# Per-page decode attention on Trainium2: the samples' softmax steps tied to pages, their small matrix products joined to the rope products, the constants and one split cut in parts

## The chip, the core and the metric

The kernel runs on one core of a Trainium2 chip. A core has five engines with instruction queues of their own: TensorE (PE, matrix products; its weight loads are listed apart as PEld), VectorE (DVE), ScalarE (ACT), GpSimd (POOL) and SyncE (SP, which here mostly issues DMAs). They meet through semaphores. The metric is the device time of one execution in microseconds (us), lower is better; the time of a kernel is the median of several runs.

## What is computed

One inference step of a one-layer decoder trunk, for a prompt of 512 tokens and, with the same weights, for 8 samples of one new token each (520 tokens in all; d_model 1024, everything float32). Each sample has 4096 past positions in 32 pages of 128, found through a page table. Cut to what the change concerns:

```python
def keys_nope(c, w_uk, k_norm_w):                 # a key per head from the 128-wide latent c
    return rmsnorm(jnp.einsum('bkr,rhd->bkhd', c, w_uk), k_norm_w)

def attend(q_nope, q_rope, k_nope, k_rope, c, w_uv, q_pos, k_pos):
    s = (jnp.einsum('bqhd,bkhd->bhqk', q_nope, k_nope)
         + jnp.einsum('bqhd,bkd->bhqk', q_rope, k_rope)).astype(jnp.float32) * SCALE
    s = jnp.where(k_pos[None, :] <= q_pos[:, None], s, -jnp.inf)
    p = jax.nn.softmax(s, axis=-1).astype(c.dtype)
    o_lat = jnp.einsum('bhqk,bkr->bqhr', p, c)
    return jnp.einsum('bqhr,rhd->bqhd', o_lat, w_uv)

# a sample: its 4096 cached latents and rope keys, then its own new token
past_c = cache_c[pages].reshape(past_len, KV_RANK)        # KV_RANK 128
past_r = cache_r[pages].reshape(past_len, QK_ROPE)        # QK_ROPE 32
c_all = jnp.concatenate([past_c, cn], axis=0)[None]

# the layer
z = hn @ w_in                        # q_lat, c_kv, k_r, u, v
sg = chunk_mix(u, v, w_s, b_s)       # the gated result, 512 wide
h = x + jnp.concatenate([attn, sg], axis=-1) @ w_o
# then a convolutional FFN (w_ff_in, w_ff_out) and a gate (w_ple_gate)
```

There are 8 heads, so a page of 128 positions gives 128 x 8 keys, each of 64 elements and normalised by its own mean square.

## The kernel before

**Arithmetic.** A large product is made of three products (`mm3`, L145 to L148): each operand is split into a rounded high part (a CAST on ACT, L135) and a remainder (a subtraction on DVE or POOL, `sub`, L130), and high x high, high x low and low x high are added in PSUM. Small products are made directly in float32, which PE does in two passes each.

**Stages.** The projections of q and the latent run to about 30 us of the span, the remaining projections and the gating to about 122, the prompt's attention in 16 blocks to about 205. Between these blocks the first sample's pages are worked on, two to a block. From 205 to 414 only pages are left, those of samples 1 to 7. From there on come the output projection (`o_half`), the FFN and the gate, to the end.

**A page** (`s_page`, L718 to L757; all 256 of them in order, 32 to a sample, 4 to a group). PE multiplies the page's latents by the key weights, six passes of 260 columns (`mm<-wuk,a`, two calls of `mm3`); 256 columns are keys, the last 4 are their products with the query. ACT squares the keys (L750) and copies the 4 columns to `raw` (L751), DVE sums the squares per head into `ss` (L752). PSUM for keys has three buffers (`mm`), the small products share two others (`ms`); the squares have three buffers, and `ss`, `raw` and the scores `sc` two each, one for each of two samples in turn. At the first page of a group the latents of a later group are split (`s_split`: CAST on ACT or POOL in turn, L714, subtraction on POOL, L130), and its rope keys are gathered by an indirect DMA that POOL issues (L588).

**Rope products.** At pages 0, 8, 16 and 24 of a sample the rope part of two groups' scores is made: 8 small products by `mm_cols` (L150 to L154), that is 16 passes on PE (`ms<-qbd,wr`), in four column tiles of 32, and one ACT copy of 64 columns into `sc` (L742).

**A sample's softmax** is a Python list of steps (`s_softmax`, L759). It is put into the list `steps` when the sample's last page has been issued, and `s_pages` (L859) takes one step from it after each page of the following sample from the fourth on: `var` (a POOL step, L792, and Ln on ACT), `rstd` (two ACT steps), the Newton correction, the sum of the scores, and the maximum per partition (all DVE); `mx_t` (L780) transposes the maxima on PE, `mx_all` reduces them on DVE, `mx_b` spreads them by a product (L789), then subtraction, Exp and sum. Behind page 23 `s_pv` (L819) issues probabilities times latents, 32 small products of 128 columns in 64 passes (L826, called PV here), and one more for the new token's own latent (L828, contraction over 8 rows of `cnew`). Then `s_out` copies that to SBUF and `s_fin` (L838) adds the four column tiles up and sums the denominators, by two `mm_cols` of 8 columns.

A scheduler sets the final order on each engine; `tc.issue_after` keeps an instruction behind another one.

**Other places.** The constants (`cst`, 128 x 1389) come in one DMA (L274), issued by SP among those of x and the first weights. The gated result `sgr` (2 tiles of 2 x 520 columns) is split for the output projection behind group 60 (L940), with the subtraction of each tile in one POOL instruction of 1040 columns. Behind the last page, what remains in `steps`, and `s_pv`, `s_out` and `s_fin` of sample 7 stand ahead of the output projection's (L968 on), the scheduler puts them among its products.

## Time and profile before

| | us |
|---|---|
| median of 3 runs (range) | 915.95 (913.79 to 916.31) |
| the profiled execution | 914.99 |
| its span, from first to last instruction | 913.1 |
| mean granted clock of PE in it | 0.991 of full |
| busy: PE, DVE, ACT, POOL | 894.5, 642.0, 505.1, 217.6 |

Everything below that names a place in time goes by microseconds from the span's start. A timeline row has the start, the busy time, engine, line, operation, and the tiles written and read; a number in brackets at its end is the idle time of the engine just before, with what ended it. Passes on PE overlap, as they are pipelined, so how fast PE goes is read from the difference between the starts of two rows, not from their durations. A group row has the number of instructions behind an x.

### The profile page before, as it was taken

How to read it: one execution, taken by the hardware profiler on the slowest of the kernel's cores; microseconds unless marked ns; L12 is line 12 of the kernel's file. 1: busy time of each engine (PE TensorE's matmuls, PEld its weight loads, DVE VectorE, ACT ScalarE, POOL GpSimd, SP SyncE). 2: the span in 40 equal slices, each digit the busy share in tenths (PEclk: the TensorE clock that was granted, in tenths of full speed). 3: DMA queues.
4: the chain of work that ended last, by engine and by line, in shares of the span. 5: the costliest groups of instructions: out<-in, count | busy, mean ns of one | idle time of the engine just before them, and what ended most of it. 6: DMA issues, size and time to landing. Idle time of an engine off the chain costs nothing.

```text
span 913.1 us, 20541 instructions
## 1 busy us (share of the span) xinstructions
PE 894.5 (98%) x7799; PEld 848.2 (93%) x7799; DVE 642.0 (70%) x1093; ACT 505.1 (55%) x1196; POOL 217.6 (24%) x240
## 2 busy tenths in 40 slices
PE   8998999999999999999999999999999999999997
PEld 6996878889999899889999999999999999999997
DVE  6679676668888898787668776337776337776775
ACT  6683368777887788785346443224443224455561
POOL 5005841238777677740000000000000000000000
PEclk9998999999999999999999999999999999999999
DMA  6332150352766556313333222322222322323311
GB/s 219 99 96 82 56 177 1 100 148 84 211 180 204 168 172 202 110 48 122 93 101 109 93 93 70 116 93 94 88 86 82 104 89 88 104 86 99 117 59 59
DMA packets 65203, 100.43 MB, mean 110 GB/s; under 512 B 13825, under 2 KB 47754, under 8 KB 65106
## 3 DMA queue, kind: packets, MB, share of 16 engines
q1 hardware_dynamic: 63058, 94.93, 32.8%
q0 software_dynamic: 2048, 4.20, 1.7%
q8 instruction: 62, 1.02, 0.5%
q14 instruction: 35, 0.29, 0.1%
HBM read 95.95 MB, written 3.15 MB: 109 GB/s over the span
## 4 chain that ended last, share of the span: by engine, by line
PE 86%; DVE 6%; ACT 3%; issue 1%; DMA 1%; SPq 1%; POOL 0%; ACTq 0%
PE mm L146 26%; PE mm L148 25%; PE mm L147 25%; DVE ss L752 2%; PE ms L826 2%; PE ms L693 1%; ACT sq L750 1%; PE ms L153 1%; ACT wr L666 1%; PE ms L146 1%; PE ms L641 1%; PE mm L658 1%; PE mm L678 1%; PE ms L148 1%; PE ms L147 1%
## 5 line engine op out<-in xcount | busy, mean ns | idle before, releaser
L146 PE MATMUL mm<-u,w 128*128 128x260 f32 x1392 | 395.1, 284 | 0.0
L148 PE MATMUL mm<-u,w 128*128 128x260 f32 x1392 | 394.5, 283 | 0.0
L147 PE MATMUL mm<-u,w 128*128 128x260 f32 x1392 | 393.5, 283 | 0.0
L147 PEld LDWEIGHTS mm<-u,w 128*128 128x128 f32 x1392 | 262.1, 188 | 0.4 <-issue 0.2
L148 PEld LDWEIGHTS mm<-u,w 128*128 128x128 f32 x1392 | 262.0, 188 | 0.1
L146 PEld LDWEIGHTS mm<-u,w 128*128 128x128 f32 x1392 | 261.8, 188 | 0.4 <-PE mm L148 0.2
L752 DVE TENSOR_REDUCE ss<-sq 128x8 f32<-128x512 f32 x256 | 168.0, 678 | 34.6 <-ACT sq L750 32.5
L130 DVE TENSOR_TENSOR w<-wr,w 128x1024 fp32r<-128x1024 f32 (+1 forms) x94 | 112.7, 1200 | 104.7 <-issue 54.1
L135 ACT CAST w<-wr 128x1024 fp32r<-128x1024 f32 (+1 forms) x94 | 96.5, 1031 | 135.9 <-PE mm L148 127.5
L750 ACT ACTIVATE sq<-mm 128x512 f32<-128x512 f32 x256 | 152.7, 609 | 25.5 <-PE mm L148 15.9
L146 PE MATMUL mm<-wuk,a 128*128 128x260 f32 x416 | 123.7, 297 | 1.8 <-ACT raw L751 1.8
L147 PE MATMUL mm<-wuk,a 128*128 128x260 f32 x416 | 118.7, 285 | 0.0
L148 PE MATMUL mm<-wuk,a 128*128 128x260 f32 x416 | 118.5, 285 | 0.0
L146 PEld LDWEIGHTS mm<-wuk,a 128*128 128x128 f32 x416 | 79.1, 190 | 4.9 <-ACT raw L751 3.1
L147 PEld LDWEIGHTS mm<-wuk,a 128*128 128x128 f32 x416 | 79.1, 190 | 0.1
L148 PEld LDWEIGHTS mm<-wuk,a 128*128 128x128 f32 x416 | 79.0, 190 | 0.0
L588 POOL DMA_INDIRECT wr<-krT,idx x64 | 62.8, 982 | 18.7 <-PE mm L678 7.4
L1069 ACT ACTIVATE a<-abuf,cst 128x512 f32<-128x512 f32 x44 | 35.9, 816 | 39.2 <-DVE abuf L1067 39.2
L130 POOL TENSOR_TENSOR a<-u,a 128x512 fp32r<-128x512 f32 x34 | 44.7, 1315 | 30.7 <-ACT a L714 28.5
L1070 DVE SCALAR_TENSOR_TENSOR a<-abuf,cst,a 128x512 f32<-128x512 f32 x44 | 33.0, 751 | 25.4 <-ACT a L1069 25.1
L751 ACT COPY raw<-mm 128x8 f32<-128x8 f32 x256 | 44.3, 173 | 0.0
L135 ACT CAST u<-a 128x520 fp32r<-128x520 f32 x24 | 14.8, 626 | 43.4 <-DVE a L1108 43.3
(306 smaller groups left out, 1341.0 us busy)
## 6 DMA issues: line engine op xcount, KB each, us to landing
wr<-w_ffi SPq DMA_DIRECT2D x44, 512.0 KB, 3.2
u<-pages SPq DMA_DIRECT2D x152, 128.0 KB, 2.6
w<-pages SPq DMA_DIRECT2D x104, 128.0 KB, 2.5
wr<-w_ffo SPq DMA_DIRECT2D x16, 512.0 KB, 3.3
wr<-w_o SPq DMA_DIRECT2D x8, 512.0 KB, 3.2
wr<-w_pg SPq DMA_DIRECT2D x8, 512.0 KB, 3.4
wr<-w_ffo SPq DMA_DIRECT2D x8, 384.0 KB
a<-xT SPq DMA_DIRECT2D x8, 260.0 KB, 6.2
```

The source lines that it names most:

```text
L130: return (nc.vector if eng == "v" else nc.gpsimd).tensor_sub(dl, src, dh.bitcast(F32))
L135: nc.scalar.copy(dh, src)
L146: nc.tensor.matmul(out, lh, rh, start=start, stop=False)
L147: nc.tensor.matmul(out, lh, rl, start=False, stop=False)
L148: return nc.tensor.matmul(out, ll, rh, start=False, stop=stop)
L588: nc.gpsimd.indirect_dma_start(krT[:, g * 128:(g + 1) * 128], None, I["krT"], bass.IndirectOffsetOnAxis(ap=idx.bitcast(U32)[:, b * 8 + g:b ...
L750: squares.append(nc.scalar.activation(u3(sq, 2, 256), ps[:, :, 0:256], AF.Square))
L751: nc.scalar.copy(raw[:, c * 8:c * 8 + 8].rearrange("p (a h) -> p a h", a=2), ps[:, :, 256:260])
L752: nc.vector.tensor_reduce(ss[:, c * 8:c * 8 + 8], sq.rearrange("p (h d) -> p h d", d=DN), axis=AX.X, op=ALU.add)
L826: nc.tensor.matmul(po[q:q + 32, 0:128], scp[:, c * 8:c * 8 + 32], pg[c // 4][:, c % 4, 128:256], start=(c < 4), stop=(c >= 29), tile_posit ...
L1069: nc.scalar.activation(c[:, 0:T], a[:, 2:T + 2], AF.Identity, scale=cw[:, m, 2:3], bias=cw[:, m, 3:4])
L1070: nc.vector.scalar_tensor_tensor(c[:, 0:T], a[:, 1:T + 1], cw[:, m, 1:2], c[:, 0:T], op0=ALU.mult, op1=ALU.add)
```

## The change

Six edits.

1. `KRQ` goes from 2 to 4: rope products are made at pages 0 and 16 of a sample only, for four groups at once, 16 products in 32 passes, held behind the preceding page's keys, with one ACT copy of 128 columns.
2. `steps` is a dict from page to step (page 4 `var`, 5 `rstd`, 6 to 9 the DVE steps, 17 `mx_all`, 20 `mx_b`, 21 subtraction, 23 Exp, 24 sum, 27 `s_pv`, 29 `s_out`).
3. `mx_t` is called by the rope products of page 16, right behind them, and `s_fin` by those of page 0 of the next sample but one, through the dict `with_qbd`.
4. The new token's product moves from `s_pv` to `s_fin`: `cnew` is padded with zeros to 128 rows and `mm_cols` adds four products of 8 columns to the same PSUM tile. PV's first product is held behind the keys before it.
5. The constants come in two DMAs, 685 columns behind all of x and the first weights, and 704 behind these.
6. The split of `sgr` goes in four pieces of 520 columns, behind groups 51, 54, 59 and 62.

```diff
-KRQ = 2
+KRQ = 4
+SGS = (51, 54, 59, 62)
...
-    def mm_cols(out, lhsT, rhs):
+    def mm_cols(out, lhsT, rhs, start=True, stop=True):
...
-        if j == 1:
-            nc.sync.dma_start(cst, I["cst"])
+    nc.sync.dma_start(cst[:, 0:NEARLY], I["cst"][:, 0:NEARLY])
...
+    nc.sync.dma_start(cst[:, NEARLY:], I["cst"][:, NEARLY:])
...
-    cnew = const([8, 128], F32, "cnew")
+    cnew = const([128, 128], F32, "cnew")
+    nc.gpsimd.memset(cnew, 0.0)
...
             for i in range(KRQ):
-                mm_cols(pr[:, 32 * i:32 * i + 32], krT[:, (g + i) * 128:(g + i + 1) * 128],
-                        qbd[:, b].rearrange("p j h -> p (j h)"))
+                with ExitStack() as es:
+                    if kmms:
+                        es.enter_context(tc.issue_after(kmms[-1].ins))
+                    r = mm_cols(pr[:, 32 * i:32 * i + 32], krT[:, (g + i) * 128:(g + i + 1) * 128],
+                                qbd[:, b].rearrange("p j h -> p (j h)"))
+            f = with_qbd.pop(g * 4, None)
+            if f:
+                f(r)
...
-        def mx_t():
+        def mx_t(after=None):
             hold["t"] = ms()
-            after_keys(lambda: nc.tensor.transpose(hold["t"][:8, 0:128], m1[:, 0:8], ident))
+            with tc.issue_after((after or kmms[-1]).ins):
+                nc.tensor.transpose(hold["t"][:8, 0:128], m1[:, 0:8], ident)
...
+        with_qbd[16] = mx_t
+        steps.update({
+            4: var,
+            5: rstd,
...
+            27: lambda: s_pv(b),
+            29: lambda: s_out(b),
+        })
...
-            nc.tensor.matmul(po[q:q + 32, 0:128], scp[:, c * 8:c * 8 + 32], pg[c // 4][:, c % 4, 128:256],
-                             start=(c < 4), stop=(c >= 29), tile_position=(0, q))
-        nc.tensor.matmul(po[0:32, 0:128], scp[:8, 256:288], cnew, start=False, stop=True, tile_position=(0, 0))
-        bst[b] = (po, psum)
+            with ExitStack() as es:
+                if c == 0:
+                    es.enter_context(tc.issue_after(kmms[-1].ins))
+                nc.tensor.matmul(po[q:q + 32, 0:128], scp[:, c * 8:c * 8 + 32], pg[c // 4][:, c % 4, 128:256],
+                                 start=(c < 4), stop=(c >= 28), tile_position=(0, q))
+        bst[b] = (po, psum, scp)
+        with_qbd[0] = lambda after: s_fin(b, after)
...
-        with tc.issue_after(kmms[-1].ins):
-            mm_cols(pt_[:, 0:8], ol, sel)
+        with tc.issue_after(after.ins):
+            mm_cols(pt_[:, 0:8], ol, sel, stop=False)
+        mm_cols(pt_[:, 0:8], cnew, scp[:, 256:264], start=False)
         mm_cols(pt_[:, 8:16], ones, psum[:, 0:8])
...
-            if steps and cur[0] % 32 > 3:
-                f = steps.pop(0)
-                if f:
-                    f()
+            f = steps.pop((cur[0] - 1) % 32, None)
+            if f:
+                f()
...
-        if g == 5:
-            s_pv(b - 1)
-            steps.extend([None, lambda b=b: s_out(b - 1), None, None, lambda b=b: s_fin(b - 1)])
...
-        if n == 60:
-            sgh, sgl = split_all(sgr, "g")
+        if n in SGS:
+            i, k = divmod(SGS.index(n), 2)
+            if k == 0:
+                sgh += pair(1, F32R)
+                sgl += pair(1, F32R)
+            split(sgh[i][:, k], sgl[i][:, k], sgr[i][:, k], l="g")
```

What this moves, word for word from the order of instructions on an engine. A row has the line, the operation, the tile written, the tiles read, and the shape; an x count folds equal rows. `mm` is a key PSUM tile, `wuk` the key weights, `a` a page's split latents, `ms` a PSUM tile of the small products, `wr` the gathered rope keys.

PE before the change, in the pages of sample 5: the transpose of sample 4's maxima (L782) stands alone between two pages' keys.

```order
L147 MATMUL mm_5380<-wuk_568,a_5148 128x260
L148 MATMUL mm_5380<-wuk_567,a_5149 128x260
L782 MATMUL ms_5356<-cst,s_5130 8x128
L146 MATMUL mm_5393<-wuk_567,a_5148 128x260
L147 MATMUL mm_5393<-wuk_568,a_5148 128x260
```

And a few pages on, at page 16, the rope products of two groups (L153), alone again.

```order
L147 MATMUL mm_5415<-wuk_568,a_5148 128x260
L148 MATMUL mm_5415<-wuk_567,a_5149 128x260
L153 MATMUL ms_5446<-qbd,wr_4739 32x32 x8
L146 MATMUL mm_5456<-wuk_567,a_5228 128x260
L147 MATMUL mm_5456<-wuk_568,a_5228 128x260
```

PE after the change at page 16 of sample 5 (L149 to L151 are `mm3`'s lines there, L156 is `mm_cols`): four groups' rope products and the transpose, L794, stand in one place.

```order
L150 MATMUL mm_5403<-wuk_570,a_5126 128x260
L151 MATMUL mm_5403<-wuk_569,a_5127 128x260
L156 MATMUL ms_5433<-qbd,wr_4730 32x32 x16
L794 MATMUL ms_5450<-cst,s_5108 8x128
L149 MATMUL mm_5453<-wuk_569,a_5228 128x260
L150 MATMUL mm_5453<-wuk_570,a_5228 128x260
```

The transpose has moved from a gap of its own to the rope products' gap, which holds twice as many of them.

PE before, behind page 23 of sample 5: the end of sample 4's PV, the new token's product (L828), and the rope products of page 24.

```order
L826 MATMUL ms_5566<-u_4593,sc_4533 32x128 x4
L826 MATMUL ms_5566<-w_4662,sc_4533 32x128 x4
L828 MATMUL ms_5566<-cnew,sc_4533 32x128
L153 MATMUL ms_5619<-qbd,wr_4739 32x32 x8
L146 MATMUL mm_5629<-wuk_567,a_5376 128x260
L147 MATMUL mm_5629<-wuk_568,a_5376 128x260
```

PE after, at page 0 of sample 5: four groups' rope products, then the final sums of sample 3, with the new token's product (`cnew`) among them.

```order
L151 MATMUL mm_5096<-wuk_565,a_4810 128x260
L156 MATMUL ms_5135<-qbd,wr_4730 32x32 x16
L156 MATMUL ms_5152<-cst,sq_5083 32x8 x4
L156 MATMUL ms_5152<-sc_3892,cnew 32x8 x4
L156 MATMUL ms_5152<-s_4490,ones 32x8 x4
L149 MATMUL mm_5169<-wuk_569,a_4894 128x260
L150 MATMUL mm_5169<-wuk_570,a_4894 128x260
```

The new token's product has left PV's end, the rope products of page 24 are gone from there, and the final sums no longer have a gap of their own.

POOL before, in the first pages of sample 7: a piece of the gated result's split (`u` 128x1040) and then, behind others, the variance step of sample 6 (L792).

```order
L130 TENSOR_TENSOR u_6713<-u_1036,u_6712 128x1040
L130 TENSOR_TENSOR a_6312<-u_6125,a_6311 128x512
L588 DMA wr_5981<-krT,idx 128x128
L714 CAST a_6390<-u_6222 128x512
L1056 MEMSET abuf_7543 128x2
L1056 MEMSET abuf_7545 128x2
L130 TENSOR_TENSOR a_6391<-u_6222,a_6390 128x512
L588 DMA wr_5981<-krT,idx 128x128
L792 TENSOR_SCALAR ss_5773<-ss_5773 128x256
```

POOL after, the same place (L133 is `sub`, L804 the variance step): two pieces of 520 columns.

```order
L133 TENSOR_TENSOR u_6643<-u_1039,u_6642 128x520 x2
L719 CAST a_6372<-u_6190 128x512
L1069 MEMSET abuf_7541 128x2
L1069 MEMSET abuf_7543 128x2
L133 TENSOR_TENSOR a_6373<-u_6190,a_6372 128x512
L735 MEMSET sc_6378 128x24
L736 COPY sc_6378<-snall 128x8
L592 DMA wr_5970<-krT,idx 128x128
L804 TENSOR_SCALAR ss_5750<-ss_5750 128x256
```

The piece of 1040 columns ahead of the variance step has become two of 520, the other two pieces lie earlier, and the set-up of `sc` (L735, L736) has moved to there.

More of the change, by code (lines that the diff above doesn't have):

```diff
@@ L34 @@
 NCONST = 1389
+NEARLY = 685
 NEG = -1.0e30
@@ L111, in trunk_step @@
     ident = take(128)
+    sel = take(8)
+    sel_last = take(8)
+    assert off[0] == NEARLY
     trilT = take(128)
@@ L115, in trunk_step @@
     row8 = take(272)
-    sel = take(8)
-    sel_last = take(8)
     gqk8 = row8[:8, 0:128].rearrange("p (a d) -> p a d", a=2)
@@ L404, in trunk_step @@
             qlat[t] = q
-    nc.gpsimd.tensor_copy(cnew, ctok[:8, 4])
+    nc.gpsimd.tensor_copy(cnew[:8], ctok[:8, 4])
     w5 = "p (t f) -> p t f"
@@ L701, in trunk_step @@
     bst = {}
+    steps, with_qbd = {}, {}
     def s_split(n):
@@ L756, in s_page @@
                 pages[b] = (None, pg)
-                steps.extend(s_softmax(b))
+                s_softmax(b)
     def s_softmax(b):
@@ L835, in s_out, with s_fin @@
             nc.scalar.copy(ol, po[:, 0:128])
-        bst[b] = (ol, psum)
-    def s_fin(b):
-        ol, psum = bst.pop(b)
+        bst[b] = (ol, psum, scp)
+    def s_fin(b, after):
+        ol, psum, scp = bst.pop(b)
         pt_ = ms()
-        with tc.issue_after(kmms[-1].ins):
-            mm_cols(pt_[:, 0:8], ol, sel)
+        with tc.issue_after(after.ins):
+            mm_cols(pt_[:, 0:8], ol, sel, stop=False)
+        mm_cols(pt_[:, 0:8], cnew, scp[:, 256:264], start=False)
         mm_cols(pt_[:, 8:16], ones, psum[:, 0:8])
@@ L846, in s_fin @@
         nc.vector.tensor_mul(olT[:, :, b], pt_[:, 0:8], rc[:, 0:8])
-    cur, steps = [0], []
+    cur = [0]
     def split_all(tiles, l):
@@ L928, in trunk_step @@
     k_pg = [wq_add(I["w_pg"][m], 1024) for m in range(8)]
+    sgh, sgl = [], []
     while cur[0] < 256:
@@ L966, in o_half @@
                 last(m, xv)
-    for f in steps:
-        if f:
-            f()
-    s_pv(7)
-    s_out(7)
-    s_fin(7)
+    with_qbd.pop(0)(kmms[-1])
+    steps[16] = with_qbd.pop(16)
+    for k in sorted(steps):
+        steps[k]()
+    with_qbd.pop(0)(kmms[-1])
     ps = ms()
```

38 lines of the change are left out of this document (14 added, 24 removed).

## The prediction

> **What bounds the kernel now.** I read the profile's first page, then the chain of waits, then PE's timeline around each small product in the sample stage.
>
> ```profile
> span 913.1 us, 20541 instructions
> PE 894.5 (98%) x7799; PEld 848.2 (93%) x7799; DVE 642.0 (70%) x1093; ACT 505.1 (55%) x1196; POOL 217.6 (24%) x240
> PE 86%; DVE 6%; ACT 3%; issue 1%; DMA 1%; SPq 1%; POOL 0%; ACTq 0%
> ```
>
> PE is busy for 98% of the span and makes up 86% of the chain. Only what shortens PE's own line can shorten the kernel: fewer passes, fewer pauses between passes, or a wait of PE. "Busy" hides pauses, since the records of pipelined passes overlap; they show in the starts. The chain in order of time gives the rhythm of the sample stage, by each sample's probability-times-latent product (PV, L826):
>
> ```profile
> 224.97 1.89 PE ms L826 x64
> 372.81 1.88 PE ms L826 x62
> 405.60 1.88 PE ms L826 x64
> 424.80 1.89 PE ms L826 x64
> ```
>
> From PV(0) at 224.97 to PV(5) at 372.81 lie five periods, 29.57 us each. The sixth, to 405.60, is 32.79, which is 3.22 more for the same work. One regular period by engine, and the rhythm of passes around one rope batch:
>
> ```profile
> 263.60:293.10 29.50, 29.00 (x348) 26.93 (x341) 24.93 (x45) 23.90 (x79) 21.31 (x24) 1.00 0.73 214
> 269.49 0.28 PE L148 MATMUL mm<-wuk,a 128*128 128x260 f32 x1
> 269.70 0.33 PE L153 MATMUL ms<-qbd,wr 128*32 128x32 f32 x16
> 269.96 0.39 PE L146 MATMUL mm<-wuk,a 128*128 128x260 f32 x1
> 270.18 0.28 PE L147 MATMUL mm<-wuk,a 128*128 128x260 f32 x1
> 270.30 0.29 PE L148 MATMUL mm<-wuk,a 128*128 128x260 f32 x1
> ```
>
> The first row gives the window, its length, then busy time of PE, PEld, DVE, ACT and POOL, the clock, the DMA share and GB/s. DVE is next behind PE, 24.93 of 29.50. Key passes start 0.12 apart (270.18 to 270.30). Across the rope batch the second pass behind it (270.18) starts 0.69 after 269.49, where two steps would be 0.24: the break costs 0.45. I price all breaks in this way, last key pass before to the second one behind.
>
> **The change part by part.**
>
> *Joined small products.* The same measure at a batch of 8 passes (sample 6's last), at the transpose of the maxima (L782), at the two early passes of PV, at the new token's product with the rope batch behind it, and at the final sums (s_fin):
>
> ```profile
> 397.80 0.27 PE L153 MATMUL ms<-qbd,wr 128*32 128x32 f32 x8
> 397.99 0.39 PE L146 MATMUL mm<-wuk,a 128*128 128x260 f32 x1
> ...
> 273.52 0.28 PE L148 MATMUL mm<-wuk,a 128*128 128x260 f32 x1
> 274.30 0.27 PE L782 MATMUL ms<-cst,s 128*8 128x128 f32 x1 [0.50 <-DVE s L805]
> 274.40 0.36 PE L146 MATMUL mm<-wuk,a 128*128 128x260 f32 x1
> 274.60 0.29 PE L147 MATMUL mm<-wuk,a 128*128 128x260 f32 x1
> ...
> 281.80 0.28 PE L148 MATMUL mm<-wuk,a 128*128 128x260 f32 x1
> 282.01 0.41 PE L826 MATMUL ms<-u,sc 128*32 128x128 f32 x2
> 282.57 0.28 PE L147 MATMUL mm<-wuk,a 128*128 128x260 f32 x1
> ...
> 285.85 0.40 PE L828 MATMUL ms<-cnew,sc 8*32 8x128 f32 x2
> 286.18 0.33 PE L153 MATMUL ms<-qbd,wr 128*32 128x32 f32 x16
> 286.44 0.39 PE L146 MATMUL mm<-wuk,a 128*128 128x260 f32 x1
> ...
> 290.00 0.28 PE L148 MATMUL mm<-wuk,a 128*128 128x260 f32 x1
> 290.22 0.25 PE L153 MATMUL ms<-cst,sq 128*32 128x8 f32 x8
> 290.30 0.23 PE L153 MATMUL ms<-s,ones 128*32 128x8 f32 x8
> 290.69 0.28 PE L147 MATMUL mm<-wuk,a 128*128 128x260 f32 x1
> ```
>
> From the start of a rope batch to the next key pass it is 0.26 with 16 passes (269.70 to 269.96) and 0.19 with 8 (397.80 to 397.99): 0.009 for a pass, so nearly all of a break is for going over and back, not for what is done there. Breaks of a regular period before: rope batches at pages 0, 8 and 16, 3 x 0.45; the transpose 1.08 - 0.24 = 0.84, of which 0.50 is a wait for DVE; the early PV passes 0.77 - 0.24 = 0.53, less 0.06 that two passes cost inside PV's own run (1.88 for 62); the token's product 0.33 and the rope batch behind it 0.26; the final sums 0.69 - 0.24 = 0.45. Together 3.70.
>
> After the change two such places are left. At page 0 there are 32 rope passes and 24 of the final sums (8 more for the new token, now in s_fin): 0.45 + 40 x 0.009 = 0.81. At page 16 there are 32 rope passes and the transpose: 0.45 + 16 x 0.009 + 0.10 (274.30 to 274.40) = 0.69. Together 1.50, so 2.20 is saved in a regular period. Pinning PV's first pass behind the keys keeps its 64 passes in one run; the break of mx_b stays.
>
> [...]
>
> *What is late next.* The steps of the softmax, on DVE and ACT, stand on the same pages as before, give or take one; pages now come faster, 24.93 of DVE work in about 27.4. Where DVE trails, a key product waits for a free PSUM buffer. Pauses that are taken from pages 0 to 15 (0.45 at page 8 and 0.84 at the transpose) may come back there, as waits: between 0 and 1.29. I take 0.30, nearer to nothing, because in the regular period PE shows a single wait, 0.50, and DVE still has 9% to spare. Net 1.90 a period.
>
> *The rope copies* go from four of 64 columns to two of 128 on ACT, with 23.90 busy of 29.50: nothing. A batch now needs four gathers of rope keys rather than two:
>
> ```profile
> 282.76 0.95 POOL L588 DMA_INDIRECT wr<-krT,idx  x1
> wr<-krT,idx POOLq DMA_INDIRECT x64, 2.9
> ```
>
> The fourth of the next sample is issued at 282.76 and lands some 2.9 later, at 285.7; that sample's page 0 is at 293.1, the end of the window quoted. 7 us to spare: 0.
>
> *The gated result's split.* Here lies the sixth period's surplus:
>
> ```profile
> 379.36 2.45 POOL L130 TENSOR_TENSOR u<-u,u 128x1040 fp32r<-128x1040 f32 x1 [3.23 <-DMA wr<-w_o]
> 387.40 0.41 POOL L792 TENSOR_SCALAR ss<-ss 128x256 f32<-128x256 f32 x1
> ...
> 389.37 0.39 PE L146 MATMUL mm<-wuk,a 128*128 128x260 f32 x1 [1.63 <-ACT raw L751]
> ...
> 391.20:394.60 3.40, 3.40 (x18) 3.40 (x18) 3.40 (x7) 2.74 (x9) 3.16 (x4) 0.50 0.57 176
> ```
>
> A piece of 1040 columns keeps POOL for 2.45, so sample 6's variance step (L792) comes late; ACT stands in order behind it with its copies, PE waits 1.63 for one, and from 391.20 runs 3.4 us at half clock (0.50 in the window's row), which loses half of them, 1.7. The two make 3.33, about the 3.22. In the new order two pieces of 520 columns (as much together) still stand ahead of that step, but earlier pieces are out of the way; a `w` split (L130, DVE) also comes into sample 7's pages. I take 2.2 of the 3.22, and keep 0 and 3.22 as ends. PV(6) isn't split before (x64), so this period gains 1.90 - 0.47 = 1.43 besides.
>
> [...]
>
> *Edges.* Sample 1's pages 0 to 23: PV(0) isn't split before either (x64), so two joins, (0.90 - 0.59) + (0.79 - 0.69), and the wait where there is one, 0.50, less 0.30: I take 0.7. Sample 0: four batches become two, 1.80 - 1.18 = 0.6, some of it hidden while the prompt's attention waits: 0.4. Behind the last page the new token's product goes, 0.33, and one `w` split has been moved ahead: 0.3.
>
> *Constants in two parts.*
>
> ```profile
> a<-xT SPq DMA_DIRECT2D x8, 260.0 KB, 6.2
> 4.52 0.43 SPq L274 DMA_DIRECT2D cst<-cst  x1
> 9.69 0.33 SPq L190 DMA_DIRECT2D wr<-w_qkr  x1
> 19.54 1.12 ACT L137 ACTIVATE w<-wr,cst 128x384 fp32r<-128x384 f32 x2 [0.77 <-DMA wr<-w_uq]
> 8.06 0.89 PE mm L256 x2
> ```
>
> The constants leave SP behind the last w_qkr rather than at 4.52, so at about 10.1, and by a landing like xT's 6.2 are there at 16.3; the first reader starts at 19.54. xT's last parts come earlier, but from 8.06 on PE has work without a break. So 0 on either side, with 3.2 to spare.
>
> Sum: 5 x 1.90 + (1.43 + 2.2) + 0.7 + 0.4 + 0.3 = 14.5. The profiled execution took 914.99 (span 913.1), 0.96 under the median of the runs, 915.95. So 900.5 on the first, and 901.4 on the median's scale, which is the forecast.
>
> **The rivals.** A difference of 0.3%, some 2.7 us, is about what a measurement of this kernel can tell from none.
>
> *DVE becomes the bound.* All of the 1.29 comes back in each period: (1.29 - 0.30) x 6.6 periods (samples 1 to 7, the first in part) = 6.5, so 907.9. For it: 24.93 of 27.4, and the transpose already waits for DVE. Against: 9% is left to it, and backlog in the early pages can be worked off in the late ones.
>
> *The pieces still delay the variance step.* That the split in four doesn't do what it says: the two pieces ahead of it still hold POOL for 2.4, as long as the one before. Then 2.2 is not gained: 903.6.
>
> [...]
>
> [...]
>
> *The constants are late.* Two transfers behind each other, 2 x 6.2, land at 22.5, 3.0 behind the first reader: 904.4.
>
> *Slower.* DVE's backlog in pages 4 to 15 makes PE wait 1.63 or more in each of samples 1 to 7, and each time the clock halves for 3.4 us as it did at 391.2: 3.2 x 7 = 22.4 against the 14.5 + 0.30 x 6.6 = 16.5 without any such wait, so 5.9 slower, 921.9. It decides from 2.4 a sample; waits of 0.50 left the clock alone in every period, so such a wait must reach between 0.50 and 1.63.
>
> **How the numbers follow.** Forecast 0.58, DVE as bound 0.15, pieces 0.12, half clock 0.04, passes 0.04, constants 0.02, slower 0.03; and 0.02 for DVE and passes together, which leaves no change. So faster by over 0.3% has 0.95, same 0.02, slower 0.03. The forecast's own ends: 1.0 for the sixth period's other end and 0.30 x 6.6 = 2.0 for no backlog at all give 898.4; with a little for pauses that I priced too high as well as too low, 897.5. Upwards the range takes in the first rival with its 907.9: 897.5 to 908.5. Left out are the passes, the slower case and the joint one.
>
> **What would show it.** Right: PV starts about 27.7 apart; rope groups of 32 with a break of 0.6 to 0.8 at pages 0 and 16 and none at 8; the transpose with no wait; no half clock about 390. Wrong: waits of PE for ACT's `raw` copies in each sample with DVE over 95% busy (DVE as bound); POOL's variance step for sample 6 late again (pieces); breaks above 1.2 at the joined places (passes); PE waiting at about 20 (constants).

## The result, and the profile after

| us | before | after |
|---|---|---|
| runs, median (range) | 915.95 (913.79 to 916.31) | 904.25 (903.94 to 907.90) |
| ratio after / before | | 0.9886, 95% interval 0.9857 to 0.9916 |
| profiled execution, its span | 914.99, 913.1 | 907.90, 906.0 |
| the changed kernel in a second job, median, ratio there | | 905.20, 0.9891 (0.9876 to 0.9905) |

The change makes the kernel faster by 1.1%, 9.7 to 11.7 us by the medians, where 14.5 were forecast (901.4, range 897.5 to 908.5). The first page of the profile after has, in the same order as before, the span, the engines and the chain:

```profile
span 906.0 us, 20621 instructions
PE 884.8 (98%) x7847; PEld 843.4 (93%) x7847; DVE 645.2 (71%) x1093; ACT 503.6 (56%) x1182; POOL 215.0 (24%) x243
PE 77%; DVE 7%; ACT 6%; issue 4%; DMA 3%; SPq 3%; POOL 1%; ACTq 0%; POOLq 0%; DVEq 0%
```

PE is still 98% busy, with some 10 us less work, and a smaller part of the chain: DVE and ACT now end waits of PE. The joined places, first page 0 of sample 3, then page 16:

```profile
262.25 0.28 PE L151 MATMUL mm<-wuk,a 128*128 128x260 f32 x1
262.46 0.46 PE L156 MATMUL ms<-qbd,wr 128*32 128x32 f32 x32
262.74 0.24 PE L156 MATMUL ms<-cst,sq 128*32 128x8 f32 x6
...
263.07 0.39 PE L149 MATMUL mm<-wuk,a 128*128 128x260 f32 x1
263.29 0.28 PE L150 MATMUL mm<-wuk,a 128*128 128x260 f32 x1
...
275.64 0.28 PE L151 MATMUL mm<-wuk,a 128*128 128x260 f32 x1
275.85 0.46 PE L156 MATMUL ms<-qbd,wr 128*32 128x32 f32 x32
276.24 0.27 PE L794 MATMUL ms<-cst,s 128*8 128x128 f32 x1
276.27 0.36 PE L149 MATMUL mm<-wuk,a 128*128 128x260 f32 x1
276.47 0.28 PE L150 MATMUL mm<-wuk,a 128*128 128x260 f32 x1
```

Page 0: 1.04 - 0.24 = 0.80 (0.81 forecast). Page 16: 0.83 - 0.24 = 0.59 (0.69), and the transpose L794 waits for nothing. 32 rope passes fill 0.39 up to the transpose. Now the waits of PE, from the view of waits (total, times, longest):

```profile
PE mm L149 <- ACT raw L762: 2.9, 10, 0.8
PE ms L801 <- DVE s L798: 1.9, 1, 1.9
PE ms L794 <- DVE s L818: 0.5, 1, 0.5
```

Windows that each hold one sample's pages, from the first key product of its page 0 to that of the next sample's, for samples 4, 6 and 7 before (the columns are the window, its length, busy time of PE, PEld, DVE, ACT and POOL, the clock, the DMA share and GB/s):

```profile
293.10:322.75 29.65, 29.13 (x351) 27.02 (x341) 25.04 (x45) 23.81 (x79) 21.37 (x24) 1.00 0.60 174
352.31:381.93 29.62, 29.11 (x350) 27.05 (x342) 24.68 (x44) 24.35 (x79) 21.40 (x23) 1.00 0.52 166
381.93:414.22 32.29, 30.48 (x327) 28.32 (x325) 27.10 (x46) 26.15 (x80) 15.75 (x16) 0.95 0.26 80
```

And for the same three samples after:

```profile
291.18:319.28 28.10, 27.86 (x356) 26.41 (x348) 25.01 (x45) 23.59 (x78) 21.28 (x24) 1.00 0.65 195
347.38:379.62 32.24, 29.65 (x356) 28.01 (x348) 27.48 (x45) 25.03 (x81) 25.66 (x27) 0.95 0.56 167
379.62:407.86 28.24, 27.45 (x299) 25.87 (x291) 27.15 (x46) 24.61 (x75) 12.04 (x16) 1.00 0.28 104
```

Sample 4 is a regular one: 29.65 has become 28.10. The long window before, 32.29 with a clock of 0.95, was sample 7's. After, sample 7 takes 28.24, and sample 6 is the long one: 32.24, again with a clock of 0.95. The half clock hasn't gone, it came one sample earlier. DVE's timeline at that place in the profile after:

```profile
363.23 0.27 DVE L797 TENSOR_REDUCE s<-ms 8x1 f32<-8x128 f32 x1
363.43 1.26 DVE L763 TENSOR_REDUCE ss<-sq 128x8 f32<-128x512 f32 x2
364.62 2.33 DVE L798 TENSOR_SCALAR s<-cst,s 8x8 f32<-8x8 f32 x1
366.87 0.67 DVE L763 TENSOR_REDUCE ss<-sq 128x8 f32<-128x512 f32 x1
```

POOL's at the same time:

```profile
364.40 1.31 POOL L133 TENSOR_TENSOR u<-u,u 128x520 fp32r<-128x520 f32 x1
365.67 1.25 POOL L133 TENSOR_TENSOR a<-u,a 128x512 fp32r<-128x512 f32 x1
367.08 0.96 POOL L592 DMA_INDIRECT wr<-krT,idx  x1 [0.16 <-issue]
```

PE's row that waits for it:

```profile
367.00 0.38 PE L801 MATMUL ms<-s,ones 8*128 8x8 f32 x2 [1.86 <-DVE s L798]
```

And the window behind that:

```profile
367.30:370.70 3.40, 3.40 (x16) 3.38 (x16) 2.45 (x5) 1.03 (x3) 0.74 (x1) 0.50 0.64 185
```

A step of 8 x 8 elements that belongs to mx_all (L798) takes 2.33 us. It ends at 366.95, when the second of two POOL subtractions that leave no gap ends (366.92); the first of these (`u` 128x520) is a piece of the gated result's split. PE waits 1.86 for it at mx_b (L801) and then runs 3.4 us at half clock. Adding all samples up, by the page starts in the trace:

| us | before | after, first profile | after, second profile | forecast change |
|---|---|---|---|---|
| start to sample 1's page 0 | 205.05 | 206.63 | 205.10 | -0.4 |
| sample 1 | 29.01 | 28.34 | 28.35 | -0.7 |
| samples 2 to 5, mean | 29.56 | 28.10 | 28.09 | -1.90 |
| sample 6 | 29.62 | 32.24 | 32.24 | -1.90 |
| sample 7, to its last key product | 32.29 | 28.24 | 27.76 | -3.63 |
| from there to the end | 498.88 | 498.16 | 498.24 | -0.3 |

### The profile page after: what moved, and what is told of

It reads as the page before. It is cut to its first block, busy times and chain, and to the rows that moved or that the text cites. A ratio compares the mean times of both kernels' runs of the same rounds, so it can differ in the third digit from the quotient of the medians.

```text
span 906.0 us, 20621 instructions
## 1 busy us (share of the span) xinstructions
PE 884.8 (98%) x7847; PEld 843.4 (93%) x7847; DVE 645.2 (71%) x1093; ACT 503.6 (56%) x1182; POOL 215.0 (24%) x243
## 4 chain that ended last, share of the span: by engine, by line
PE 77%; DVE 7%; ACT 6%; issue 4%; DMA 3%; SPq 3%; POOL 1%; ACTq 0%; POOLq 0%; DVEq 0%
PE mm L149 23%; PE mm L150 23%; PE mm L151 23%; DVE ss L763 2%; SPq L605 2%; PE ms L838 1%; ACT sq L761 1%; ACT wr L670 1%; PE ms L697 1%; PE ms L149 1%; DMA wr<-w_u 1%; PE ms L151 1%; PE ms L150 1%; DVE wr L673 1%; PE ms L156 1%
## 5 line engine op out<-in xcount | busy, mean ns | idle before, releaser
L149 PE MATMUL mm<-u,w 128*128 128x260 f32 x1392 | 395.2, 284 | 0.1
L151 PE MATMUL mm<-u,w 128*128 128x260 f32 x1392 | 394.7, 284 | 0.0
L151 PEld LDWEIGHTS mm<-u,w 128*128 128x128 f32 x1392 | 262.8, 189 | 0.2 <-issue 0.2
L149 PEld LDWEIGHTS mm<-u,w 128*128 128x128 f32 x1392 | 262.5, 189 | 0.5 <-PE mm L151 0.2
L133 DVE TENSOR_TENSOR w<-wr,w 128x1024 fp32r<-128x1024 f32 (+1 forms) x94 | 112.6, 1199 | 106.1 <-issue 54.0
L763 DVE TENSOR_REDUCE ss<-sq 128x8 f32<-128x512 f32 x256 | 166.8, 678 | 26.4 <-ACT sq L761 21.9
L149 PE MATMUL mm<-wuk,a 128*128 128x260 f32 x416 | 123.4, 297 | 2.5 <-ACT raw L762 2.1
L151 PE MATMUL mm<-wuk,a 128*128 128x260 f32 x416 | 118.4, 285 | 0.0
L149 PEld LDWEIGHTS mm<-wuk,a 128*128 128x128 f32 x416 | 79.1, 190 | 8.2 <-ACT raw L762 6.3
L151 PEld LDWEIGHTS mm<-wuk,a 128*128 128x128 f32 x416 | 79.0, 190 | 0.0
L133 POOL TENSOR_TENSOR a<-u,a 128x512 fp32r<-128x512 f32 x34 | 44.2, 1301 | 17.0 <-ACT a L719 15.0
```

What stands on the lines that cost most here:

```text
L133: return (nc.vector if eng == "v" else nc.gpsimd).tensor_sub(dl, src, dh.bitcast(F32))
L149: nc.tensor.matmul(out, lh, rh, start=start, stop=False)
L151: return nc.tensor.matmul(out, ll, rh, start=False, stop=stop)
L763: nc.vector.tensor_reduce(ss[:, c * 8:c * 8 + 8], sq.rearrange("p (h d) -> p h d", d=DN), axis=AX.X, op=ALU.add)
```

## The experiments

All of these were compared with the kernel before in the same job. "Period" is from the first pass of one sample's PV to that of the next; the mean is over the four from PV(0) to PV(4), then come sample 6's pages (to PV(5)) and sample 7's (to PV(6)). The rows are of three jobs, in which the kernel before took 914.92 (again, constants in one, late split, steps spread), 915.52 (two groups, step on ACT, pinned, steps early) and 915.22 (the other four). Across jobs I compare ratios and periods, as medians can differ by 0.6 for that alone.

| kernel | median us (range) | ratio, 95% interval | mean period | to PV(5) | to PV(6) |
|---|---|---|---|---|---|
| changed, again | 905.20 (904.58 to 905.90) | 0.9891 (0.9876 to 0.9905) | 28.09 | 32.28 | 28.55 |
| constants in one | 907.31 (904.73 to 910.54) | 0.9924 (0.9905 to 0.9942) | 28.12 | 32.28 | 28.52 |
| split late, whole | 901.66 (899.46 to 901.97) | 0.9847 (0.9834 to 0.9860) | 28.09 | 28.12 | 30.85 |
| steps spread | 908.54 (907.54 to 909.76) | 0.9931 (0.9919 to 0.9944) | 29.60 | 29.20 | 29.22 |
| two groups | 907.06 (905.09 to 908.32) | 0.9900 (0.9883 to 0.9916) | 28.31 | 32.51 | 29.01 |
| mx_all's step on ACT | 902.21 (900.18 to 903.30) | 0.9847 (0.9829 to 0.9865) | 28.10 | 28.78 | 28.59 |
| pieces pinned | 903.58 (903.39 to 904.59) | 0.9867 (0.9848 to 0.9886) | 28.10 | 28.81 | 30.09 |
| steps early | 899.84 (899.54 to 900.95) | 0.9826 (0.9809 to 0.9842) | 27.62 | 29.31 | 28.41 |
| early, step on ACT | 901.20 (900.22 to 901.62) | 0.9847 (0.9831 to 0.9863) | 27.62 | 29.33 | 28.44 |
| the same, constants in one | 903.09 (901.61 to 903.63) | 0.9866 (0.9846 to 0.9886) | 27.63 | 29.34 | 28.41 |
| early, two groups | 902.32 (901.98 to 905.24) | 0.9871 (0.9852 to 0.9890) | 27.82 | 30.57 | 29.21 |
| token's product back | 905.75 (903.81 to 906.48) | 0.9896 (0.9878 to 0.9913) | 28.36 | 31.02 | 29.08 |

**The changed kernel again**, unaltered.

> The changed kernel once more, unaltered. In its first profile one 8x8 step of mx_all on DVE (L798) took 2.33 us in sample 6 where the seven others took 0.21, PE waited 1.9 for it and ran 3.4 us at half clock; that execution took 907.9, the other three about 904.1. Theory: this meeting of POOL's two subtractions with that step is a matter of the moment, and the usual execution has neither the wait nor the half clock: profile 903 to 905, period from PV(5) to PV(6) near 28.1 to 29. Rival: it is in every execution, and what differs between the runs lies elsewhere: profile again near 907 with a step above 2 us, period above 32. On either theory the other periods stay at 28.07 and the median within 903.5 to 905.

The answer of the trace for L798 there (shortest, median, longest in ns):

```profile
L798 DVE TENSOR_SCALAR s<-cst,s x8: 207/209/2348, 221.8 to 412.9; 8x8 f32<-8x8 f32 x8
```

My theory fell: the long step is in this execution too (2.35), at the same place, with the same period of 32.28, and in three later kernels that keep the pieces and the steps (constants in one, two groups, token's product back) PE waits 1.9 for it again. It is part of the change, and the scatter between the runs lies elsewhere: sample 1's page 0 came 1.5 earlier than in the first profile.

**Constants in one DMA**, at the old place.

```diff
+        if j == 1:
+            nc.sync.dma_start(cst, I["cst"])
-    nc.sync.dma_start(cst[:, 0:NEARLY], I["cst"][:, 0:NEARLY])
...
-    nc.sync.dma_start(cst[:, NEARLY:], I["cst"][:, NEARLY:])
```

> As changed, but the constants come in one DMA at the old place, among x and the first weights. In the changed kernel's first profile w_u's first part was cast at 28.60 rather than 26.66, PE waited 1.2 at the rstd product (L341), ran at half clock from 36.2 to 39.6, and page 0 came 0.91 later than before. Theory A (my term of 0 was wrong): the new place of the constants causes it, so w_u's cast is back near 26.7, no wait at L341, and the time falls by 0.5 to 1.5 below the changed kernel's, 902.7 to 903.7. Theory B (a landing that differs from run to run): no difference, within 0.5 of the changed kernel.

Neither. Page 0 came 0.5 earlier (124.69, against 125.21 of the kernel beside it), and the median was 2.1 longer, with ranges that overlap; from the last key product to the end it took 499.63 rather than 498.24. A second pair, below, repeats the difference behind the last key product.

**The split late and whole.**

```diff
-        if n in SGS:
...
+        if n == 60:
+            sgh, sgl = split_all(sgr, "g")
```

> As changed, but the gated result is split as before the change, whole, behind group 60. Theory A (the pieces are what freed sample 7, worth 2.2 as forecast): the wait of PE for a raw copy above 1.5 us and 3.4 us of half clock are back in sample 7's pages, and the time is 2 to 3.3 above the changed kernel's, about 906.2 to 907.5. Theory B: the pieces only carry POOL's load from sample 7 to sample 6, where they hold mx_all: sample 6's period is 28.1 here, and the sum is within 1 of the changed kernel.

B, and more than it said. POOL's timeline of this kernel in sample 7:

```profile
375.91 2.45 POOL L133 TENSOR_TENSOR u<-u,u 128x1040 fp32r<-128x1040 f32 x1
378.44 0.40 POOL L804 TENSOR_SCALAR ss<-ss 128x256 f32<-128x256 f32 x1
```

PE's:

```profile
379.89 0.39 PE L149 MATMUL mm<-wuk,a 128*128 128x260 f32 x1 [1.29 <-ACT raw L762]
```

And the window of the half clock:

```profile
381.60:385.00 3.40, 3.40 (x18) 3.40 (x17) 3.40 (x7) 2.74 (x8) 2.15 (x2) 0.50 0.09 27
```

The stall of sample 7 is back, as A said (a wait of 1.29 and the half clock), but sample 6's 32.28 has become 28.12, and the two periods make 58.97 against 60.83. Without its sixth edit the change is faster by 3.5 (901.66 to 905.20, ranges apart). The two periods hold 1.9 of that. Another 1.3 lies behind the last key product (496.96 to the end, 498.24 in the changed kernel), where neither theory looked: passes start closer there, which the last experiment comes back to.

**Steps spread** over pages 6 to 14.

```diff
-            7: lambda: newton(raw, ss, raw, t),
-            8: lambda: nc.vector.tensor_add(sc[:, 0:256], sc[:, 0:256], raw),
-            9: lambda: nc.vector.tensor_reduce(m1[:, 0:8], s3.rearrange("p c h -> p h c"), axis=AX.X, op=ALU.max),
+            8: lambda: nc.vector.scalar_tensor_tensor(t, ss, -0.5, t, op0=ALU.mult, op1=ALU.mult),
+            10: lambda: nc.vector.scalar_tensor_tensor(raw, t, 1.5, raw, op0=ALU.add, op1=ALU.mult),
+            12: lambda: nc.vector.tensor_add(sc[:, 0:256], sc[:, 0:256], raw),
+            14: lambda: nc.vector.tensor_reduce(m1[:, 0:8], s3.rearrange("p c h -> p h c"), axis=AX.X, op=ALU.max),
```

> As changed, but the softmax's DVE steps of pages 6 to 9 stand on pages 6, 8, 10, 12 and 14 (the two Newton steps apart); all are still ahead of the transpose at page 16. Theory A: the 0.4 by which a period fell short of the forecast, and the 0.3 that I had allowed, are DVE's backlog in pages 8 to 15 (PE waits there for raw copies, about 1.0 a period), and it arises because a step on every page asks more of DVE than a page of PE lasts: periods fall from 28.07 to 27.1 to 27.4 and the time by 4 to 7, to 897 to 900. Theory B: DVE has 25.1 us of work in a period and lacks room wherever the steps stand: the waits move to other pages, and the gain is under 2.

The view of waits of this kernel, at the transpose:

```profile
PE ms L794 <- DVE s L819: 7.1, 7, 1.3
```

Neither theory had this: the period went up to 29.60, since the transpose of the maxima now waits 1.0 on average in each of seven samples. The maximum is called at page 14, DVE is far behind PE there, and the scheduler moved the transpose out of page 16's gap into one of its own, 2.9 us further on, with a break of 1.56 in sample 3. By its time it isn't a test of the backlog, since I had put the last step too close to its reader. The pauses of PE ahead of that place say something, though: they make 1.0 in sample 3, at the same pages as in the changed kernel, although the second Newton step and the sum have moved away. The two steps ahead of them still take 0.89 and 0.92, as in the changed kernel (0.90 and 0.91); the next experiment shows why this matters. One more thing it shows by the way: samples 6 and 7 ran without a half clock, 29.20 and 29.22 (the clock is 1.00 from 347.38 to 407.86).

**Steps early**: one page earlier, and apart where there is room.

```diff
-            4: var,
-            5: rstd,
...
-            9: lambda: nc.vector.tensor_reduce(m1[:, 0:8], s3.rearrange("p c h -> p h c"), axis=AX.X, op=ALU.max),
+            3: var,
+            4: rstd,
+            5: lambda: nc.vector.tensor_mul(raw, raw, y0),
+            6: lambda: nc.vector.scalar_tensor_tensor(t, ss, -0.5, t, op0=ALU.mult, op1=ALU.mult),
+            8: lambda: nc.vector.scalar_tensor_tensor(raw, t, 1.5, raw, op0=ALU.add, op1=ALU.mult),
+            9: lambda: nc.vector.tensor_add(sc[:, 0:256], sc[:, 0:256], raw),
+            11: lambda: nc.vector.tensor_reduce(m1[:, 0:8], s3.rearrange("p c h -> p h c"), axis=AX.X, op=ALU.max),
```

> As changed, but the softmax steps start one page earlier and stand further apart: var 3, rstd 4, product 5, Newton's two steps 6 and 8, sum 9, maximum 11 (where the last try had the maximum at 14, and the transpose waited 1.1 to 1.3 for it in every sample). Theory A (a step on every page makes the backlog, and 3 pages of DVE's lag must lie between maximum and transpose): waits for raw copies in pages 8 to 15 fall from 1.0 to below 0.4 a period, the transpose waits less than 0.3, periods 27.3 to 27.8, time 2 to 5 lower than the changed kernel's. Theory B (DVE has too much work in pages 4 to 16 for any order that is ready by page 16): what the raw copies no longer wait, the transpose does; periods 28.0 to 28.6.

A, by its numbers. The periods are 27.62 (27.67 was forecast for the change itself), and the time falls to 899.84, the best of all kernels here. A regular sample keeps one pause of PE in its early pages, 0.45 with the way back into the rhythm, where the changed kernel has three that make 1.0. DVE's timeline in the changed kernel, in sample 3, with the reductions of pages 6 to 8:

```profile
269.34 0.90 DVE L815 TENSOR_TENSOR raw<-raw,g 128x256 f32<-128x256 f32 x1
270.17 0.67 DVE L763 TENSOR_REDUCE ss<-sq 128x8 f32<-128x512 f32 x1
270.77 0.91 DVE L160 SCALAR_TENSOR_TENSOR g<-ss,g 128x256 f32<-128x256 f32 x1
271.61 0.67 DVE L763 TENSOR_REDUCE ss<-sq 128x8 f32<-128x512 f32 x1
272.20 0.41 DVE L161 SCALAR_TENSOR_TENSOR raw<-g,raw 128x256 f32<-128x256 f32 x1
272.53 0.67 DVE L763 TENSOR_REDUCE ss<-sq 128x8 f32<-128x512 f32 x1
```

A reduction and a step on each page: 269.34 to 272.53 hold two steps with a reduction each and one step more, 3.2 us, or 0.9 to 1.4 for a page that PE does in 0.72. That is the backlog, and an earlier start with more room between steps takes 0.47 off each period.

More than the order changed, though. The first two steps take 0.90 and 0.91, where the third, of the same shape, takes 0.41. POOL's timeline in the changed kernel at the same time:

```profile
269.34 0.62 POOL L719 CAST a<-u 128x512 fp32r<-128x512 f32 x1
270.04 1.36 POOL L133 TENSOR_TENSOR a<-u,a 128x512 fp32r<-128x512 f32 x1
```

And the same two steps with the steps early, in sample 3:

```profile
266.63 0.41 DVE L815 TENSOR_TENSOR raw<-raw,g 128x256 f32<-128x256 f32 x1
267.56 0.52 DVE L816 SCALAR_TENSOR_TENSOR g<-ss,g 128x256 f32<-128x256 f32 x1
```

In the changed kernel both end some 0.3 behind a POOL instruction that runs beside them; a page earlier they mostly miss POOL. DVE's busy time in sample 4 falls by 0.85 with them, from 25.01 to 24.16. So the gain of 0.47 may come from the order, or from meeting POOL less. No run here sets the two apart; the steps spread, with more room but the same long steps and the same pauses, speak for POOL.

**Two groups** at a time again.

```diff
-KRQ = 4
+KRQ = 2
```

> As changed, but rope products again for two groups at a time, at pages 0, 8, 16 and 24; the transpose and the final sums still ride behind those of pages 16 and 0. Breaks that return: page 8, 0.45, and page 24, 0.45, less 32 passes x 0.009 that leave pages 0 and 16: +0.6 a period by the breaks alone. Theory A (PE's waits in pages 8 to 15 are DVE's backlog, and a pause in these pages is paid back by shorter waits): the break at page 8 costs nothing, so a period grows by 0.1 to 0.3 from 28.1 and the waits for raw copies fall below 0.7 a period; time +0.5 to +2. Theory B (waits and breaks add up): +0.6 a period, time +4.

A. The breaks at pages 8 and 24 are back, 0.45 and 0.46, and those at pages 0 and 16 fall to 0.68 and 0.47: by the breaks +0.66, and the period grows by 0.22, as the pauses of PE in the early pages shrink from 1.0 to 0.56. The times (ratios 0.9900 and 0.9891, intervals overlapping) can't tell the two kernels apart; the periods can. The joining of the rope products, the edit that the change is named for, is worth a third of what the breaks say: a pause at page 8 is time in which DVE catches up, and the waits behind it are shorter by as much.

**Two groups, steps early.**

> As changed, with the early steps and rope products for two groups at a time again. With the steps as changed, going back to two groups cost 0.24 a period (28.09 to 28.33) and not the 0.6 that the breaks make, since a pause at page 8 shortened the waits behind it. Theory A (refund by the backlog): with the waits gone there is little to refund, so it costs 0.4 to 0.6 a period here, 28.0 to 28.2 after 27.62, time +3 to +4 over the early steps. Theory B (a break at page 8 or 24 is cheaper than I priced it, whatever the backlog): again 0.2 to 0.3 a period, 27.9, time +1.5 to 2.

The number is B's, 0.20 (27.82 against 27.62), and yet not for B's reason: the breaks are as dear as before in this trace, +0.66 together. What paid them back is the one pause of 0.45 that the early steps had left, which is gone here. So A's mechanism holds, and I had overlooked what was left to refund.

**The token's product back** at PV's end.

```diff
+        nc.tensor.matmul(po[0:32, 0:128], scp[:8, 256:288], cnew[:8], start=False, stop=True, tile_position=(0, 0))
...
-        mm_cols(pt_[:, 0:8], cnew, scp[:, 256:264], start=False)
```

> As changed, but the new token's product stands at the end of PV again, over 8 rows, and not among the final sums. I priced it at 0.33 a period, less 8 passes x 0.009 = 0.07 that leave page 0. It stands behind page 27, where PE's line has no waits, so no refund: period 28.3 to 28.4 instead of 28.09, time +1.5 to +2.2 over the changed kernel. Rival: it hides behind the way back from PV to the keys, 0.2 in any case: +0.1 a period, time within 0.8.

```profile
285.28 0.40 PE L840 MATMUL ms<-cnew,sc 8*32 8x128 f32 x2
285.61 0.39 PE L149 MATMUL mm<-wuk,a 128*128 128x260 f32 x1
```

The period is 28.36, +0.27 as priced: two passes over 8 rows cost 0.33 here (285.28 to 285.61), as they did before the change, and no wait refunds them behind page 27. The time shows only 0.5 of the 2, as sample 6's period is 1.3 shorter: L798 takes 2.35 here too and PE waits 1.9, but no half clock follows (the clock is 1.00 from 347.38 to 379.62).

**mx_all's step on ACT.**

```diff
-            nc.vector.tensor_scalar(m2[:8, 8:16], ident[:8, 0:8], m2[:8, 0:1], None, op0=ALU.mult)
+            with tc.issue_after(squares[-1].ins):
+                nc.scalar.activation(m2[:8, 8:16], ident[:8, 0:8], AF.Copy, scale=m2[:8, 0:1])
```

> As changed, but the 8x8 scaling step of mx_all goes from DVE to ACT. Theory A (in sample 6 this DVE step is held while POOL subtracts twice without a gap, 364.40 to 366.92, and ends just behind it): on ACT it takes 0.3 or less in every sample, PE's wait of 1.9 at mx_b and the half clock near 367 are gone, period PV(5) to PV(6) 28.1 to 28.8 instead of 32.3, time 3 to 4 lower, near 901.5. Theory B (DVE is merely late there, backlog): the wait at mx_b stays, no gain.

```profile
L799 ACT ACTIVATE s<-cst,s x8: 295/296/301, 220.7 to 409.3; 8x8 f32<-8x8 f32 x8
```

A: 0.30 in every sample, no wait at mx_b, no half clock (1.00 from 347.38 to 379.62, where the changed kernel has 0.95), 28.78 instead of 32.28, and 3.0 off the median (902.21; the intervals of the two ratios lie apart). On ACT it takes 0.295 to 0.301 in all eight samples; what held it on DVE was POOL, as its end at POOL's (366.95 and 366.92) said.

**Pieces pinned** behind later splits.

```diff
-SGS = (51, 54, 59, 62)
+SGS = {51: 53, 54: 56, 59: 60, 62: 62}
...
-            split(sgh[i][:, k], sgl[i][:, k], sgr[i][:, k], l="g")
+            nc.scalar.copy(sgh[i][:, k], sgr[i][:, k])
+            with tc.issue_after(subs[SGS[n]].ins):
+                sub(sgl[i][:, k], sgr[i][:, k], sgh[i][:, k], "g")
```

> As changed, but three of the four pieces of the gated result's split have their subtraction held on POOL behind later splits of pages: the second behind the subtraction of group 56, the third and fourth behind those of groups 60 and 62, so that neither stands back to back with another one ahead of mx_all in sample 6, nor ahead of sample 6's variance step. Theory A (the pieces hurt by where they stand): no step of mx_all above 0.3, no wait at mx_b, sample 6's period 28.1 and sample 7's 28.1 to 28.5 instead of 32.3 and 28.6, time near 901. Theory B: POOL has no room for the pieces in these two samples, a wait of over 1 us of PE and a half clock appear at another page, time above 903.5.

```profile
L798 DVE TENSOR_SCALAR s<-cst,s x8: 208/209/219, 221.5 to 410.7; 8x8 f32<-8x8 f32 x8
```

Between the two. With the second piece a place further on, the step takes 0.21 in all samples and sample 6 28.81: the meeting of the two engines is the cause, shown from POOL's side now. But with the third and fourth piece moved behind sample 6's variance step, sample 7's period is 30.09. The median is 903.58, 1.6 below the changed kernel's rather than 4, and the intervals of the two ratios overlap.

**Both gains together**, and the same with the constants in one DMA.

> As changed, with both of the edits that gained: the softmax steps a page earlier and further apart, and mx_all's scaling step on ACT. If the two losses are separate (DVE's backlog in pages 8 to 15 of every sample, and POOL's two subtractions that hold the DVE step in sample 6), the gains add: periods 27.6, sample 6's 28.2 to 28.6 rather than 29.31, no wait at mx_b, time about 899, 1 below the early steps alone. Rival: the early steps had already moved mx_all away from the two subtractions (its step took 0.59), so nothing is left to gain, within 0.5 of 899.8.

> The same kernel with the constants in one DMA at the old place. The earlier try of this place, on the changed kernel, took 907.31 (904.73 to 910.54), where the changed kernel in the same job took 905.2, though its profile had page 0 earlier by 0.5. Theory A (the place of the constants does nothing to PE's line, and that difference was scatter of the start): within 0.7 of the kernel beside it. Theory B (the old place costs 2): 1.5 to 2.5 above it, and the loss lies ahead of page 0 in the profile.

The rival of the first, by its periods: they are as with the early steps alone, 29.33 against 29.31 in sample 6. The median, 901.20, is 1.4 above that kernel's in another job, more than the 0.5 that the rival allowed. The early steps had already moved mx_all to where its step takes 0.59 only (361.15 to 361.74, beside a subtraction of POOL that ends at 361.71). What sample 6 still loses, 1.7 over a regular period, begins elsewhere in both kernels: PE waits 0.86 (up to 356.32, steps early) and 0.87 (up to 356.63) for a `raw` copy. On the second B's size is right, 1.9, and its place wrong. From the last key product to the end it takes 499.81 rather than 498.28. A window of 400 us of the tail, first of the kernel with the constants in two parts:

```profile
450.00:850.00 400.00, 399.94 (x3324) 399.64 (x3323) 253.63 (x354) 164.21 (x245) 0.00 (x0) 1.00 0.29 96
```

Then of the kernel with the constants in one:

```profile
450.00:850.00 400.00, 399.96 (x3315) 399.66 (x3314) 252.89 (x352) 163.71 (x245) 0.00 (x0) 1.00 0.29 95
```

At full clock in both, PE starts 9 passes fewer of 3324 in the same time. The kernel before, with one DMA, has 3315 as well, and the first pair 3324 (in two) and 3316 (in one). The late split, with the constants in two, has 3333.

## Why the prediction was right, and where it was not

**The breaks** were right: 0.80 and 0.59 for 0.81 and 0.69, and the token's product 0.27 for 0.33 - 0.07 = 0.26. The chances give 0.04 each to a break whose cost lies in its passes and to a half clock that has another cause than the wait. No run shows either: 32 rope passes take 0.39 up to the transpose (275.85 to 276.24), and where the wait at mx_b went, on ACT and by pinning, the half clock went too.

**"I take 0.30"** of the 1.29 that might come back as waits was the first step that failed. The rows of a regular sample after show PE held behind pages 8 and 13 and in page 12; with the way back into the rhythm this makes 1.0, so the period is 28.09 and not 27.67, four times 0.4 and more over all samples. My reason, that DVE had 9% to spare, was an average over 28 us; in the early pages it has 0.9 to 1.4 us of work to PE's 0.72. The first rival was the truer one, in three quarters of its price. The early steps, the same steps at other pages, make it 27.62. That isn't order alone: two steps that meet POOL in the changed kernel take 0.9 each there and 0.4 to 0.5 a page earlier, and which of the two makes the gain isn't settled.

**"I take 2.2 of the 3.22"** was right for the place and wrong for the sum. Sample 7 gains more (4.05 and 4.53 with the regular gain, for 3.63). But the pieces that "lie earlier" were given no cost, and there they are dearer: sample 6, forecast at -1.90, became longer by 2.62. The late split shows the account: the sixth edit as a whole loses 3.5, of which 1.9 lies in samples 6 and 7 and 1.3 in the tail, where its cause is open.

**Edges.** Sample 1: 0.67 for 0.7 (the terms named there make 0.61). The start: nothing, for 0.4. In eleven profiles of kernels that share it, page 0 begins between 122.91 and 126.69, so a term of 0.4 can't be seen in the start as a whole. From page 0 to sample 1's page 0 it can, and it has the wrong sign: 79.26 before, 79.87 to 79.96 in the profiles after the change with four groups at a time, and 79.28 and 79.33 in the two with two groups. So between the blocks of the prompt's attention the joining costs 0.6, for reasons that no run here looked into. The end: 0.64 to 0.72 for 0.3, but not for the reason given, since the constants' place alone makes more than that in the two pairs; some comes back, as the first product behind the pages starts 0.52 after the last key product, where it started 0.12 after it.

**"0 on either side"** for the constants holds at the start, and fails in the tail: 1.4 and 1.5 less from the last key product on in both pairs (the medians differ by 2.1 and 1.9). Why passes start 0.3% closer when the constants came in two parts isn't settled: no wait of PE shows there, and the clock is the same. The pace goes with the kernel and not with the run (3325 and 3324 passes in the two profiles of the changed kernel), and not with the constants alone, as the late split reaches 3333.

So the total came within the range by errors of both signs. By the second profile, 9.1 of the 14.5: short by 1.7 in samples 2 to 5, by 4.5 in sample 6 and by 0.45 at the start, over by 0.9 in sample 7 and by 0.3 in the tail.

## What to carry to other kernels

A break between unlike products was priced well by the start-to-start difference across it (0.81 and 0.69 forecast, 0.80 and 0.59 measured), but before it is booked as a gain, look at the engine that trails in the same pages: a pause of PE there may be paid back in waits (breaks of +0.66 made the period +0.22 with two groups), and a step a page earlier may be worth more than the break (0.47 a period with the steps early). Work on a shared helper engine that is moved "out of the way" needs a price at its new place too, read from what the other engines do at that moment, down to the smallest step of a chain that PE waits for. And where a helper's steps differ in length though their shape is the same (0.41 and 0.90 here), look at what the other engines do beside them before the order is blamed.

## What the runs showed of the hardware

**POOL held some DVE instructions and not others.** The 8 x 8 step (L798) takes 0.21 in the other samples. It takes 0.59 and 0.89 where it meets one subtraction of POOL (steps early, steps spread), and 2.33 to 2.35 where it meets two that leave no gap (after, again, token's product back). Each time it ends some 0.03 behind the last of them: at 361.74 and 361.71, 368.15 and 368.12, 366.95 and 366.92. The 256 reductions of the pages (L763) take 0.63 to 0.70 in the profile after, whatever POOL does. The same happens to larger steps: in the changed kernel the first two softmax steps of 128 x 256, with both inputs in SBUF, take 0.90 to 0.92 in the pages of samples 2 to 6 beside a cast or subtraction of POOL, and 0.42 and 0.43 for sample 7's own softmax, where POOL is idle. The subtraction L821, with one input in PSUM, keeps 0.43 while POOL subtracts beside it for all of that time (at 252.42, with POOL at it from 251.99 to 253.27). Why the ones are held and the others aren't, no run here shows.

**A short wait was followed by half clock, or not.** Waits of PE of 1.29 (late split), 1.63 (before), 1.86 (after) and 1.89 (again) were followed by stretches at half clock: 3.4 us with a clock of 0.50 in the first three, and 0.50 from 367.00 to 370.30 in the last. A wait of 1.89 at the same place (token's product back) was not: the clock stays at 1.00 from 347.38 to 379.62. So the length of the wait alone doesn't tell the two apart. Nor does the half clock begin with the wait: before, it begins at 391.20, where the wait ended at 389.37, and after, at 367.30, where it ended at 367.00. What decides isn't shown, as no run moved a wait on purpose. That the wait has its part in it the runs show for sample 6: with the wait at mx_b the half clock went too, on ACT and by pinning (the clock is 1.00 from 347.38 to 379.62 in both, 0.95 in the changed kernel).
